# Joining the block inverses of a delta-rule layer: small products of different blocks issued in turn, matrix by matrix

## The chip, the cores and the metric

One core of one Trainium2 chip. The time is device microseconds of one execution of the whole program. The kernel before took 2122.88 us (median of three runs, 2118.37 to 2123.48).

## What is computed

A backbone with two layers over 512 latent and 256 context tokens of width 1024. Each layer has a modulation by a condition vector, an RMS norm, one input projection whose columns feed three groups of heads (latent attention, 2-D neighbourhood attention, a bidirectional gated delta rule), an output projection, and a SwiGLU. The change lies in the delta rule, in the inverse of a unit triangular matrix for every chunk, head and direction:

```
L = jnp.where(strict, jnp.einsum('bhnid,bhnjd->bhnij', kb, k) * decay, 0.0)
eye = jnp.eye(DN_CHUNK, dtype=f32)
tinv = lax.linalg.triangular_solve(L + eye, jnp.broadcast_to(eye, L.shape), left_side=True,
                                   lower=True, unit_diagonal=True)
u = tinv @ (v * beta[..., None])
w = tinv @ (kb * jnp.exp(gc)[..., None])
...
def step(S, xn):
    v_new = xn[0] - xn[1] @ S
    S_new = S * xn[3][..., None, None] + jnp.swapaxes(xn[2], -1, -2) @ v_new
```

The kernel works with chunks of 128 tokens: six chunks (four latent, two context), four heads, two directions, so 48 inverses of 128x128 a layer.

## The kernel before

The program runs on the five engines of one core under a scheduler. The Python code states tiles and operations; a list scheduler with a model of time writes the order in which each engine gets its instructions, and puts the semaphores. Code that is written in another order therefore also comes out elsewhere in the engines' lists.

Large projections split each float32 operand into a high and a low part (`wtiles`, L206, on ScalarE and GpSimd) and make three products for one (`mm3`, L107). All products are issued through `mm` (L103), so the profile shows them at L104 and tells them apart by their tiles. The small products of this change are plain float32, and each leaves two load and two matmul records in the trace.

The inverses are made in three steps. `base_inverse` (L664) inverts the 32x32 blocks on the diagonal of all matrices by substitution on VectorE and writes them to the tile `ST` ("strips"). `inverse` (L916) joins them into 128x128 inverses, first 32-blocks to 64-blocks, then 64-blocks to 128. One call takes two chunks, thus eight matrices (`R8`) in both directions, and is called for `x0` = 0, 2 and 4 in each layer: six calls in all. `scan` (L1014) then runs the recurrence over the chunks with the joined inverses `Yt`.

In `inverse` the 128 partitions hold four blocks of 32 (`B4`), or two halves of 64 (`fst`, `snd`). `LP` is the strictly triangular matrix, loaded by two transfers of four matrices each. Five groups of products follow each other, with copies out of PSUM between them:

- `pp` (L933 to L935): 32 products of 32x32, block `b` in, block `b ^ 1` out, copied to `p32` by ScalarE (L948);
- `xq` (L949 to L951; a half of the same PSUM tile as `pp`, so the profile calls it `pp<-p,strips`): 16 products of 32x32, blocks 1 and 2, copied into `X` by VectorE (L953);
- `pp64` (L958 to L960; `pp<-X,LP` in the profile): 16 products of 64x64, from one half to the other, copied to `p64` by VectorE and ScalarE (L962, L963);
- `yq` (L965 to L968): 32 products of 32x32, copied into `Y` by ScalarE (L970);
- `yq64` (L972 to L975; `yq<-Y,p`): 16 products of 64x64, each half copied into `Y` by ScalarE (L975).

In every group the loop over blocks is outermost and that over the eight matrices innermost: eight products in a row have the same rows and columns of the array, with other operands. All products of a group write one PSUM tile, each block its own partitions.

The first call in a layer runs beside the last projections (`TAIL`, `do_z`, `do_kv`, `do_ql`). The second and third run beside neighbourhood attention (`attention`, L847: `s_na`, `tp_na`, `o_na`) and the scans (`ks`, `yp`, `sp`, `qs`, `oa`), which `beside` (L1099) interleaves by a table; in layer 0 also beside the products of the modulation (`acc_ada`, from `ada_cols`, L220). `acc_ada` writes four strips of 32 columns in turn (`g = 32 * (k % 4)`). Loads for all of them are issued on SP's queue: `LP` (L922), the scan's `vp`, `kt`, `At` and `z` (L1011), `wada` (L225).

Of the kernel before, what the change touches and what calls it, by code (L numbers as in the profile page):

```python
# [102 lines left out]
def mm(nc, out, lhsT, rhs, start=True, stop=True):  # L103
    nc.tensor.matmul(out, lhsT, rhs, start=start, stop=stop)  # L104
# [16 lines left out]
def h4(t):  # L121
    return t.rearrange("p (h d) -> p h d", h=4)
# [240 lines left out]
def layer(tc, nc, a, l, es_x, xT, env, nx):  # L363
# [14 lines left out]
    def eb(name):  # L378
        tag = EB_TAG.get(name, "e")
        return psE.tile([P, 512], F32, tag=tag, name=name, bufs=EB[tag])  # L380
# [535 lines left out]
    def inverse(x0, sb, eb):  # L916


        LP = []
        for x in (x0, x0 + 1):  # L920
            LP.append(h4(sb.tile([P, 512], F32, tag="lLP", name="LP", bufs=2)))
            nc.sync.dma_start(out=LP[-1], in_=h4(d_LP[x]))  # L922
        Ys = [ST[:, 24 * d + 4 * x0:24 * d + 4 * x0 + 8] for d in range(2)]
        R8 = range(8)
        i8 = lambda t, c: t.rearrange("p (x c) -> p x c", c=c)
        f2 = lambda t: t.rearrange("p x c -> p (x c)")
        mix = sb.tile([P, 8, 32], F32, tag="mix", name="mix", bufs=1)
        for b in range(4):
            V.transpose(out=f2(mix[B4[b]]), in_=f2(Ys[b % 2][B4[b]]))
        q2 = eb("pp")  # L930
        pp, xq = i8(q2[:, 0:256], 32), i8(q2[:, 256:512], 32)
        for b in range(4):
            o = b ^ 1  # L933
            for x in R8:
                mm(nc, pp[B4[o], x], LP[x // 4][B4[b], x % 4, B4[o]], mix[B4[b], x])  # L935

        X = sb.tile([P, 8, 2, 32], F32, tag="X", name="X", bufs=1)
        for b in range(4):
            V.transpose(out=X[B4[b], :, b % 2], in_=f2(Ys[b // 2][B4[b]]))
        G.memset(X[B4[0], :, 1], 0.0)  # L940
        G.memset(X[B4[3], :, 0], 0.0)
        Y = []
        for d in range(2):
            Y.append(sb.tile([P, 8, 4, 32], F32, tag="Y", name=f"Y{d}", bufs=4 if x0 else 2))
            G.tensor_tensor(out=Y[d], in0=Ys[d].unsqueeze(2).to_broadcast([P, 8, 4, 32]),
                            in1=bm.unsqueeze(1).to_broadcast([P, 8, 4, 32]), op=ALU.mult)
        p32 = sb.tile([P, 8, 32], F32, tag="mix", name="p32", bufs=1)
        S.copy(out=p32, in_=pp)  # L948
        for b in (1, 2):  # L949
            for x in R8:  # L950
                mm(nc, xq[B4[b], x], Ys[1 - b % 2][B4[b], x], p32[B4[b], x])  # L951
        for b in (1, 2):
            V.tensor_copy(out=X[B4[b], :, 1 - b % 2], in_=xq[B4[b]])  # L953
        Xh = X.rearrange("p x b c -> p x (b c)")
        Yf = [t.rearrange("p x b c -> p x (b c)") for t in Y]
        pp = i8(eb("pp64"), 64)
        hf = ((fst, snd), (snd, fst))
        for a_, b_ in hf:  # L958
            for x in R8:
                mm(nc, pp[b_, x], LP[x // 4][a_, x % 4, b_], Xh[a_, x])  # L960
        p64 = sb.tile([P, 8, 64], F32, tag="X", name="p64", bufs=1)
        V.tensor_copy(out=p64[:, 0:4], in_=pp[:, 0:4])  # L962
        S.copy(out=p64[:, 4:8], in_=pp[:, 4:8])  # L963
        yq = i8(eb("yq")[:, 0:256], 32)
        for b in range(4):  # L965
            o = b ^ 1
            for x in R8:
                mm(nc, yq[B4[o], x], p32[B4[b], x], Ys[1 - b % 2][B4[b], x])  # L968
        for d, r, c in ((0, 0, 1), (0, 2, 3), (1, 1, 0), (1, 3, 2)):
            S.copy(out=Y[d][B4[r], :, c], in_=yq[B4[r]])  # L970
        yq = i8(eb("yq64"), 64)
        for d, (a_, b_) in enumerate(hf):  # L972
            for x in R8:
                mm(nc, yq[a_, x], p64[b_, x], Yf[d][b_, x, b_])
            S.copy(out=Yf[d][a_, :, b_], in_=yq[a_])  # L975
        for x in range(2):
            Yt[x0 + x] = [t[:, 4 * x:4 * x + 4] for t in Yf]

    es_si = ExitStack()
    sb_i = pool(es_si, f"sb_i{l}", side=B_)  # L980
    inverse(0, sb_i, att_bank)
    if "n" in TAIL[l]:
        open_na()
# [89 lines left out]
    def finish(c, tok, o):  # L1073
# [13 lines left out]
        for h in range(4):  # L1087
            PE.transpose(tp[:, HS[h]], o[:, HS[h]], ident)

        stt(out=qT[:, :, tok], in0=h4(tp), scalar=sml[:, 12:13], in1=h4(z), op0=ALU.mult, op1=ALU.mult)  # L1090

    I_, S_ = (lambda x: lambda: inverse(x, sb, eb)), (lambda d, x: lambda: scan(d, x))
    dn = iter([S_(0, 0), S_(1, 1), S_(0, 1), S_(1, 0), I_(2), S_(0, 2), S_(1, 3), I_(4), es_v.close,
               S_(0, 4), S_(1, 5), S_(0, 5), S_(1, 4), S_(0, 3), S_(1, 2)])
# [372 lines left out]
```

## Time and profile before

| | |
|---|---|
| median of three runs | 2122.88 us (2118.37 to 2123.48) |
| the profiled execution, its time | 2125.45 us |
| its span from first to last instruction | 2123.6 us |
| mean granted TensorE clock | 0.968 |
| TensorE (PE) busy | 1990.2 us, 94%, 12770 matmul records |
| VectorE (DVE) | 1172.3 us, 55% |
| ScalarE (ACT) | 714.3 us, 34% |
| GpSimd (POOL) | 758.7 us, 36% |
| 16 DMA engines, mean rate | 110 GB/s |

Busy times are shares of the whole span. Matmuls overlap each other in the array, so a matmul record is longer than the distance between two starts, and a busy PE is not a PE at its peak. In the timeline a row with "x16" is a group of 16 records, from the start of the first to the end of the last. In the chain of waits a piece counts from where the piece before it ends.

### The profile page before, as it was taken

To read this page: it belongs to the slowest core of one execution; us is meant where nothing else is said; L and a number is where in the kernel's file an instruction comes from. 1 tells how busy PE (TensorE), PEld (TensorE's weight loads), DVE (VectorE), ACT (ScalarE), POOL (GpSimd) and SP (SyncE) were. 2 spreads that over 40 slices of the span, in tenths; PEclk is the share of its full clock that TensorE was granted. 3 is DMA by queue.
4 is the path that set the end of the run, shared out by engine and by line. 5 is a ranking of instruction groups with operands and counts; after the bars stand their busy time and mean duration, and the time that the engine had idled before them with its cause. 6 is when DMAs were issued, how large, how long until landed. Compare 5 with 4: busy or idle time off the path is not lost. (4 is left out here: it accounts for less than half of the span.)

```text
span 2123.6 us, 32023 instructions
## 1 busy us (share of the span) xinstructions
PE 1990.2 (94%) x12770; PEld 1684.4 (79%) x12770; DVE 1172.3 (55%) x2045; ACT 714.3 (34%) x1385; POOL 758.7 (36%) x540
## 2 busy tenths in 40 slices
PE   6999998998998999999999988888998889999998
PEld 4788787887787888888888876767787678888887
DVE  4888813667656457246443268894568753212123
ACT  5433322334544221122122244333434543222233
POOL 3466132104322222322222443823311353444444
PEclk9999998999999999999999999999999999999999
DMA  7324252543322345344442331334232231333332
GB/s 279 82 76 153 81 157 77 168 149 112 104 64 78 109 126 165 97 130 131 128 129 76 121 95 55 119 120 124 91 88 77 87 95 60 99 99 94 95 97 92
DMA packets 119309, 232.56 MB, mean 110 GB/s; under 512 B 30516, under 2 KB 55988, under 8 KB 119032
## 3 DMA queue, kind: packets, MB, share of 16 engines
q1 hardware_dynamic: 119160, 230.51, 34.9%
q8 instruction: 101, 1.65, 0.3%
q14 instruction: 48, 0.39, 0.1%
HBM read 199.46 MB, written 31.01 MB: 109 GB/s over the span
## 5 line engine op out<-in xcount | busy, mean ns | idle before, releaser
L217 POOL TENSOR_TENSOR wl<-wr,wh 128x1024 fp32r<-128x1024 f32 (+2 forms) x188 | 442.0, 2352 | 848.4 <-ACT wh L216 834.9
L216 ACT CAST wh<-wr 128x1024 fp32r<-128x1024 f32 (+2 forms) x190 | 193.5, 1019 | 713.0 <-PE acc_gu L104 287.6
L104 PE MATMUL acc_gu<-fh,wh 128*128 128x512 f32 (+1 forms) x1024 | 359.1, 353 | 9.5 <-ACT fh L304 8.7
L104 PE MATMUL acc_gu<-fl,wh 128*128 128x512 f32 (+1 forms) x1024 | 361.0, 353 | 4.1 <-DVE fl L305 4.1
L104 PE MATMUL acc_gu<-fh,wl 128*128 128x512 f32 (+1 forms) x1024 | 360.2, 352 | 0.0
L104 PE MATMUL acc_in<-hh,wh 128*128 128x512 f32 (+1 forms) x640 | 230.5, 364 | 18.6 <-ACT xp L491 6.9
L104 PE MATMUL acc_in<-hl,wh 128*128 128x512 f32 (+1 forms) x640 | 229.9, 360 | 3.2 <-DVE hl L305 2.0
L104 PE MATMUL acc_in<-hh,wl 128*128 128x512 f32 (+1 forms) x640 | 227.3, 359 | 3.4 <-POOL wl L217 3.4
L104 PEld LDWEIGHTS acc_gu<-fh,wh 128*128 128x128 f32 x1024 | 194.1, 190 | 37.5 <-ACT fh L304 10.9
L1348 DVE TENSOR_TENSOR av<-acc_gu,av 128x768 f32<-128x768 f32 (+1 forms) x44 | 36.3, 825 | 338.4 <-PE acc_gu L104 330.0
L104 PEld LDWEIGHTS acc_gu<-fl,wh 128*128 128x128 f32 x1024 | 195.0, 190 | 30.3 <-DVE fl L305 4.3
L104 PEld LDWEIGHTS acc_gu<-fh,wl 128*128 128x128 f32 x1024 | 194.9, 190 | 26.3
L104 PEld LDWEIGHTS acc_in<-hh,wh 128*128 128x128 f32 x640 | 126.1, 198 | 45.4 <-ACT xp L491 8.6
L104 PE MATMUL acc_d<-al,wh 128*128 128x512 f32 (+1 forms) x444 | 157.2, 354 | 0.0
L104 PE MATMUL acc_d<-ah,wh 128*128 128x512 f32 (+1 forms) x444 | 157.2, 354 | 0.0
L104 PE MATMUL acc_d<-ah,wl 128*128 128x512 f32 (+1 forms) x444 | 156.1, 354 | 0.0
L254 DVE CUSTOM_DVE_ANT_0 junk<-wada,scb 128x1024 f32<-128x1024 f32 x112 | 145.3, 1297 | 6.8 <-DMA wada<-w_adaT 4.0
L104 PEld LDWEIGHTS acc_in<-hl,wh 128*128 128x128 f32 x640 | 127.0, 198 | 25.2 <-DVE hl L305 4.6
L104 PEld LDWEIGHTS acc_in<-hh,wl 128*128 128x128 f32 x640 | 126.1, 198 | 22.8 <-POOL wl L217 4.7
L1366 DVE SCALAR_TENSOR_TENSOR xT<-acc_d,mod,xT 128x512 f32<-128x512 f32 (+1 forms) x76 | 46.5, 634 | 155.2 <-PE acc_d L104 155.2
L501 DVE SCALAR_TENSOR_TENSOR cy<-xp,cw,cy 128x770 f32<-128x770 f32 (+1 forms) x96 | 117.7, 1226 | 20.5 <-ACT cy L499 18.5
L1352 DVE TENSOR_TENSOR al<-av,ah 128x768 fp32r<-128x768 f32 (+1 forms) x44 | 100.4, 2282 | 35.1 <-ACT ah L1351 35.1
(391 smaller groups left out, 3857.0 us busy)
## 6 DMA issues: line engine op xcount, KB each, us to landing
wr<-w_gu SPq DMA_DIRECT2D x88, 512.0 KB, 3.5
wada<-w_adaT SPq DMA_DIRECT2D x56, 512.0 KB, 3.4
wr<-w_in SPq DMA_DIRECT2D x48, 512.0 KB, 3.6
wr<-w_dn SPq DMA_DIRECT2D x32, 448.0 KB, 3.3
wada<-w_ada SPq DMA_DIRECT2D x24, 512.0 KB, 3.4
wada<-w_ada SPq DMA_DIRECT2D x8, 1024.0 KB, 8.1
wr<-w_dn SPq DMA_DIRECT2D x16, 512.0 KB, 3.5
xT<-xT SPq DMA_DIRECT2D x16, 384.0 KB, 4.9
```

What stands on the lines that cost most here:

```text
L104: nc.tensor.matmul(out, lhsT, rhs, start=start, stop=stop)
L216: S.copy(out=hi[:, sl], in_=raw[:, sl])
L217: eng.tensor_tensor(out=lo[:, sl], in0=raw[:, sl], in1=hi[:, sl].bitcast(F32), op=ALU.subtract)
L254: V.tensor_tensor_reduce(out=junk, in0=w, in1=scb[:, s], scale=1.0, scalar=0.0, op0=ALU.mult, op1=ALU.add, accum_out=mod[l][:, part, j, s: ...
L501: stt(out=y[:, :wid], in0=xp[:, j:j + wid], scalar=w_(j), in1=y[:, :wid], op0=ALU.mult, op1=ALU.add)
L1348: tt(out=av[:, :nT], in0=accs[1][:, :nT], in1=av[:, :nT], op=ALU.mult)
L1352: after.append(tt(out=l_[:, :nT], in0=av[:, :nT], in1=h_[:, :nT].bitcast(F32), op=ALU.subtract))
L1366: stt(out=xT[:, m, st_], in0=acc, scalar=mod[l][:, 5, m, s:s + 1], in1=xT[:, m, st_], op0=ALU.mult, op1=ALU.add)
```

## The change

In the five groups the loops change places: the matrices `x` are outermost and the blocks innermost, so that neighbouring products belong to different blocks. In `yq64` the two copies come after all 16 products, not each after its eight. Products, operands, tiles and transfers stay the same.

```diff
@@ -929,9 +929,10 @@
         q2 = eb("pp")
         pp, xq = i8(q2[:, 0:256], 32), i8(q2[:, 256:512], 32)
-        for b in range(4):
-            o = b ^ 1
-            for x in R8:
+
+        for x in R8:
+            for b in range(4):
+                o = b ^ 1
                 mm(nc, pp[B4[o], x], LP[x // 4][B4[b], x % 4, B4[o]], mix[B4[b], x])
@@ -946,8 +947,8 @@
         S.copy(out=p32, in_=pp)
-        for b in (1, 2):
-            for x in R8:
+        for x in R8:
+            for b in (1, 2):
                 mm(nc, xq[B4[b], x], Ys[1 - b % 2][B4[b], x], p32[B4[b], x])
@@ -955,23 +956,24 @@
         hf = ((fst, snd), (snd, fst))
-        for a_, b_ in hf:
-            for x in R8:
+        for x in R8:
+            for a_, b_ in hf:
                 mm(nc, pp[b_, x], LP[x // 4][a_, x % 4, b_], Xh[a_, x])
...
         yq = i8(eb("yq")[:, 0:256], 32)
-        for b in range(4):
-            o = b ^ 1
-            for x in R8:
+        for x in R8:
+            for b in range(4):
+                o = b ^ 1
                 mm(nc, yq[B4[o], x], p32[B4[b], x], Ys[1 - b % 2][B4[b], x])
...
         yq = i8(eb("yq64"), 64)
+        for x in R8:
+            for d, (a_, b_) in enumerate(hf):
+                mm(nc, yq[a_, x], p64[b_, x], Yf[d][b_, x, b_])
         for d, (a_, b_) in enumerate(hf):
-            for x in R8:
-                mm(nc, yq[a_, x], p64[b_, x], Yf[d][b_, x, b_])
             S.copy(out=Yf[d][a_, :, b_], in_=yq[a_])
```

How it moves TensorE's instructions is read from the order in which the two built programs list them. First, TensorE in layer 0, the end of the first joining, beside the projection of a z tile; `yq_2653` is `yq64`, `Y_2572` and `Y_2574` are the two directions. Before:

```order
L104 MATMUL acc_in<-hh_125,wl 128x512
L104 MATMUL yq_2653<-Y_2572,p_2613 64x64 x8
L104 MATMUL acc_in<-hh_126,wh 128x512
L104 MATMUL acc_in<-hl_134,wh 128x512
L104 MATMUL acc_in<-hh_126,wl 128x512
```

Now:

```order
L104 MATMUL acc_in<-hh_125,wh 128x512
L104 MATMUL acc_in<-hl_133,wh 128x512
L104 MATMUL acc_in<-hh_125,wl 128x512
L104 MATMUL yq_2653<-Y_2572,p_2613 64x64
L104 MATMUL yq_2653<-Y_2574,p_2613 64x64
```

Before, the eight products of the second direction stood 22 products of the projection further down. Now the two directions alternate, one product each, and all 16 stand together ahead of `acc_in<-hh_126`.

Second, TensorE in layer 1, the start of the second joining, beside attention and scans; `pp<-mix` is `pp`, `pp<-p_13967` is `xq`, `pp_13987` is `pp64`. Before:

```order
L104 MATMUL pp<-mix,LP 32x32 x22
L104 MATMUL sp<-w,kt 128x128 x4
L104 MATMUL pp<-mix,LP 32x32 x10
L889 MATMUL tp_na<-cst_61,pr 128x128 x8
L104 MATMUL yp<-vp,Y_13119 128x128 x4
L104 MATMUL pp<-p_13967,strips 32x32 x14
L104 MATMUL o_na<-pt,nav 64x128
L104 MATMUL pp<-p_13967,strips 32x32 x2
```

Now:

```order
L104 MATMUL yp<-vp,Y_13117 128x128 x4
L104 MATMUL pp<-mix,LP 32x32 x32
L104 MATMUL sp<-w,kt 128x128 x4
L889 MATMUL tp_na<-cst_61,pr 128x128 x8
L104 MATMUL pp<-p_13967,strips 32x32 x16
L104 MATMUL yp<-vp,Y_13119 128x128 x4
L104 MATMUL o_na<-pt,nav 64x128 x8
L104 MATMUL pp_13987<-X,LP 64x64 x16
```

The scan's `sp` stood inside `pp` and now follows it; `xq` and `pp64` stand unbroken, and `yp` comes after `xq`. Elsewhere in the two attention stretches pieces of the joining and of the scans change places in the same way.

## Rows read from the trace of the kernel before

**Rows 1.** The page: engines' busy times, and the chain by engine.

```profile
PE 1990.2 (94%) x12770; PEld 1684.4 (79%) x12770; DVE 1172.3 (55%) x2045; ACT 714.3 (34%) x1385; POOL 758.7 (36%) x540
...
PE 29%; DVE 6%; POOL 1%; ACT 1%; DMA 1%; issue 1%; SPq 0%; DVEq 0%; ACTq 0%; POOLq 0%
```

**Rows 2.** Busy time by stretch: length, busy us of each engine (instructions), clock, DMA.

```profile
281.00:375.00 94.00, 83.76 (x655) 70.92 (x654) 29.41 (x71) 27.14 (x58) 29.67 (x16) 0.85 0.37 107
375.00:470.00 95.00, 95.00 (x1234) 79.60 (x1233) 64.12 (x214) 33.09 (x115) 11.93 (x19) 1.00 0.49 158
...
1525.00:1592.00 67.00, 63.69 (x792) 56.36 (x793) 45.48 (x112) 24.92 (x73) 17.37 (x14) 0.95 0.32 97
```

**Rows 3.** Chain of waits, 1470 to 1600 us: start, us, engine, tile, line.

```profile
1479.90 1.84 PE pp L104 x64
...
1486.72 1.02 PE pp L104 x32
...
1492.73 1.83 PE pp L104 x32
1494.56 1.84 PE yq L104 x64
...
1503.19 1.07 PE yq L104 x16
...
1509.41 1.07 PE yq L104 x16
```

**Rows 4.** TensorE's waits, 1525 to 1592 us: total us, times, longest.

```profile
PE sp L104 <- DVE w L1035: 2.8, 1, 2.8
```

**Rows 5.** TensorE's waits, 318 to 376 us.

```profile
PE tr_ada L104 <- DVE adarow L231: 4.3, 2, 3.8
PE ms_q L104 <- DVE sqs L775: 3.5, 1, 3.5
```

**Rows 6.** Timeline, groups of small products: start us, us, operation, tiles, count.

```profile
295.09 1.91 PE L104 MATMUL pp<-mix,LP 32*32 32x32 f32 x64
...
301.60 1.09 PE L104 MATMUL pp<-p,strips 32*32 32x32 f32 x32
...
306.21 1.90 PE L104 MATMUL pp<-X,LP 64*64 64x64 f32 x32
...
379.44 0.50 PE L104 MATMUL pp<-mix,LP 32*32 32x32 f32 x10
...
386.28 0.37 PE L104 MATMUL pp<-mix,LP 32*32 32x32 f32 x6
...
416.78 1.02 PE L104 MATMUL yq<-Y,p 64*64 64x64 f32 x14
...
418.63 0.32 PE L104 MATMUL yq<-Y,p 64*64 64x64 f32 x2
...
420.36 1.14 PE L104 MATMUL yq<-Y,p 64*64 64x64 f32 x16
```

**Rows 7.** Timeline, products on four column strips and on the full array.

```profile
339.98 0.30 PE L104 MATMUL acc_ada<-wada,sc 128*32 128x128 f32 x1
...
339.98 0.32 PE L104 MATMUL acc_ada<-wada,sc 128*32 128x128 f32 x4
...
377.01 0.64 PE L104 MATMUL acc_ada<-wada,sc 128*32 128x128 f32 x16
...
1563.33 1.16 PE L104 MATMUL yp<-rr,Y 128*128 128x128 f32 x8
```

**Rows 8.** Busy time in two stretches at a lower clock, columns as in rows 2.

```profile
310.32:313.73 3.41, 3.41 (x14) 3.05 (x13) 0.13 (x1) 2.74 (x7) 0.44 (x1) 0.50 0.00 0
...
1498.16:1501.57 3.41, 3.41 (x10) 2.63 (x9) 0.34 (x2) 3.37 (x5) 0.00 (x0) 0.50 0.01 2
```

**Rows 9.** Groups by shape, 1470 to 1600 us: busy us, mean ns of one record.

```profile
L104 PE MATMUL pp<-mix,LP 32*32 32x32 f32 x192 | 6.6, 197 | 0.0
...
L104 PE MATMUL pp<-X,LP 64*64 64x64 f32 x96 | 6.1, 222 | 0.0
```

## Prediction

> **What bounds the kernel now.** I read the page first, then the busy time by stretch around the six joinings, then the chain of waits there, then TensorE's waits, and last the timeline of the small products. On the page TensorE is busy 94% of the span and has the largest share of the chain that ended last [rows 1]. That is a mean over stages, so the stretches decide. The second and third joining of layer 0 lie in 375 to 470 us, where TensorE is busy 95.00 of 95.00 us and VectorE 64.12; those of layer 1 lie in 1525 to 1592, with TensorE at 63.69 of 67.00 us and VectorE at 45.48. The first joining of each layer stands among projections; for layer 0 that is 281 to 375 us [rows 2]. In layer 1 the chain shows the products of the first joining themselves: 1.84 + 1.02 + 1.83 + 1.84 + 1.07 + 1.07 = 8.67 us of the chain for one joining [rows 3]. Six joinings run, so some 52 us of chain are at stake: TensorE is what ends last, and shorter products there should shorten the span. The limits of this: TensorE waits 2.8 us for VectorE's w in 1525 to 1592 [rows 4], and 4.3 and 3.5 us for VectorE after the first joining of layer 0 [rows 5].
>
> **What the small products cost now.** Each float32 product leaves two records, so `pp` with 32 products is a group of 64. Groups of one block give the pace within a block: 6 records take 0.37 us and 10 take 0.50, so a further record costs 0.13 / 4 = 0.0325 us. For 64-blocks, 2 records take 0.32 us and 14 take 1.02: 0.058 us each [rows 6]. All of `pp` at the pace of one block would take 0.50 + 54 x 0.0325 = 2.25 us, but its row says 1.91. It holds three passages from one block to the next, so each saves 0.34 / 3 = 0.115 us, the time of 3.5 records. Products of two blocks thus already run beside each other at a passage, 7 records in the time of 3.5, which is 0.016 us a record. The two blocks differ in rows and in columns of the array and write other partitions of the same PSUM tile.
>
> A row for four at once is `acc_ada`, whose products go in turn to four 32-column strips: 16 records with 128 columns take 0.64 us and four take 0.32, so 0.32 / 12 = 0.027 us a record. `yp`, on the full array with the same 128 columns, takes 8 records in 1.16 us, about 0.12 a record. The first record of an `acc_ada` group takes 0.30 us and the first four together 0.32, so starts 0.007 us apart are possible [rows 7].
>
> **The change, term by term.** Nothing is added or removed: 112 products for each joining before and after. The scheduler cuts them into 63 groups by the order listing, as many as before. What changes is that neighbours now belong to different blocks. If each block keeps its pace and the blocks run beside each other, a group lasts as long as one block's share of it, plus a step of 0.007 us for each further block.
> - `pp` (32 products, four blocks): one block has 16 records, 0.50 + 6 x 0.0325 = 0.70 us, with three steps 0.72. Against 1.91: 1.19 us saved.
> - `xq` (16 products, two blocks): 0.70 against 1.09: 0.39.
> - `pp64` (16 products, two halves): a half has 16 records, 1.14 us, with its step 1.15. Against 1.90: 0.75.
> - `yq` (32 products, four blocks, 64 records as in `pp`): 1.19.
> - `yq64`: two groups of 1.07 us on the chain become one of 1.08 [rows 3]: 1.06.
>
> That is 4.58 us for a joining and 27.5 us for six. The unknown is how closely four blocks can follow each other when a record is only 0.0325 us long. No row of before has that. Its bounds: the starts 0.007 us apart of `acc_ada` allow the full 27.5. At the 0.016 us of the passages, `pp` and `yq` would be 64 x 0.016 and the 0.197 us of a record [rows 9], 1.22 us, and save 0.69 each, in all 3.58, for six 21.5 us. At the 0.027 us that `acc_ada` keeps up, they would save nothing (64 x 0.027 + 0.197 = 1.92), `xq` 0.04, and the 64-blocks, two at 0.058 and so 0.029 us a record, all of theirs: 1.85, for six 11.1 us. I take 27.5, because the four strips of `acc_ada` are the row nearest in the number of neighbours, and their pace there is what one strip's 128 columns need.
>
> Edits that cost nothing here: the copies of both halves of `yq64` on ScalarE now wait for all 16 products, at most 0.6 us later than the first did. ScalarE is busy 33.09 of 95.00 us there [rows 2], and the first reader, a scan's `yp`, stands several products further on TensorE. If that cover is gone it costs 0.6 us a joining, 3.6 in all. With matrices outermost, the second of the two loads of `LP` is first needed halfway through `pp` instead of after four products, so SP's queue gets a little more time. Transfers of the scans (`vp`, `kt`, `At`) change places with those of `LP` and `w_ada` on SP as TensorE gets on faster; no wait for one of these is among TensorE's largest [rows 4, 5].
>
> From 27.5 I give back 3 us, the size of the 2.8 us wait on VectorE [rows 4]: with 9.2 of the 67 us gone from layer 1's stretch (two joinings), the scan's way through VectorE is what comes late next. That leaves 24.5 us. The profiled execution took 2125.45 us (span 2123.6), so 2101.0 by its own time. It lies 2.6 us above the median of the runs, 2122.88, so the forecast for the median is **2098.4 us**.
>
> **What the clock may add.** After `pp64` and `yq` of the first joining, the granted clock is 0.50 from 310.32 to 313.73 us and, in layer 1, from 1498.16 to 1501.57 [rows 8]. That is the lower of the two levels (1.2 and 2.4 GHz), each time after 1.83 + 1.84 us of small products [rows 3]. With that stretch cut to half, the fall may not come: each is worth half of 3.41, 1.7 us, together 3.4. I leave it out of the sum and in the range.
>
> **The rivals.**
>
> *Starts cannot follow closer than about 0.027 us.* For it: that is the steady pace of `acc_ada`, and nothing in the trace is steadily faster. Against it: passages at 0.016 us, and starts at 0.007. It gives 11.1 us, so 2111.8. The Trainium skill, "TensorE: Matmul & The Clock Gate", Part 1, says that starts of matmuls never come below about 25 ns however few columns they have. The passages of this trace lie below that, but only for a few records at a time.
>
> *The new order gives the gain back.* The list that TensorE follows is written by a scheduler, and in the two attention stretches it is a different one: scan products stand earlier or later between the pieces of the joining. A scan product whose VectorE input is late holds up all that stands behind it. The price of one such wait is 2.8 to 4.3 us [rows 4, 5], so seven new ones would eat the 24.5. Against it: TensorE loses hardly anything in 375 to 470 us now, and VectorE has 30.88 us free there. The time would lie within 6.4 us of before, about 2120. It also stands for the case that the scheduler does not keep the blocks in turn within `pp`, `xq` and `yq`, which the listing's names do not show.
>
> *Blocks of different rows cannot write one PSUM tile at once.* Then each product waits for the one before it to end. A record lasts 0.197 us for 32-blocks and 0.222 for 64-blocks [rows 9], so a product would take 0.197 + 0.0325 = 0.23 us instead of 1.91 / 32 = 0.06, and 0.28 instead of 0.119: 80 x 0.17 + 32 x 0.16 = 18.7 us more for a joining, 112 for six, 2235 us. It makes the kernel slower from the point at which one passage costs more than the next product gains. Against it stands the 0.115 us that each passage of `pp` saves, with all blocks in one PSUM tile. The Trainium skill, "TensorEngine Tiling (Array Packing)", Restrictions and Gotchas, states this rule: different row tiles cannot access the same PSUM bank simultaneously. The passages of this trace speak against it.
>
> **How the numbers follow.** Chances: forecast 0.58, starts at 0.027 us 0.18, gain given back 0.18, blocks shutting each other out 0.06. The range goes down to 27.5 + 3.4 for the clock + 3 for a kinder order, 34 us, so 2089, and up through the second case with 6 us given back to the order, to 2118. It leaves out the last case and most of the third. Measurement can tell 0.3%, 6.4 us. Faster by more than that: 0.58 + 0.18 + 0.02 of the third case = 0.78. Within it: 0.13 of the third. Slower: the remaining 0.03, and 0.06: 0.09.
>
> **What would show it.** In the timeline after, an unbroken `pp` or `yq` of 64 records should take about 0.7 us instead of 1.91, `pp64` and `yq64` of 32 about 1.15. If `pp` takes about 1.2, the pace of the passages holds for four; if 1.9, the second case; if far more, the last. The stretch from the first attention product to the last scan should shrink by some 10 us in each layer; if the groups shrink and the stretch does not, new waits for VectorE should stand before `sp`, `yp` or `s_na`. The half-clock stretches after the first joining should be gone. The forecast is wrong if the groups shrink as said and the time does not follow within 6 us.

## The result, and the profile after

The changed kernel takes 2106.43 us, median of four runs (2104.68 to 2107.70); the kernel before, beside it, 2122.14 (four runs, 2118.37 to 2123.48). The ratio is 0.9924 with a 95% interval of 0.9903 to 0.9945: 15.7 us faster, where 24.5 were forecast (2098.4). The profiled execution took 2107.7 us, with a span of 2105.9: 17.7 us less than the span before. The page of the kernel after, TensorE's busy time and the chain by engine, to be held against [rows 1]:

```profile
PE 1960.6 (93%) x12770; PEld 1656.1 (79%) x12770; DVE 1183.1 (56%) x2045; ACT 714.5 (34%) x1385; POOL 760.6 (36%) x540
...
PE 27%; DVE 7%; DMA 2%; ACT 2%; POOL 1%; issue 1%; SPq 0%; DVEq 0%; ACTq 0%; POOLq 0%
```

The records are the same in number. TensorE is busy for 29.6 us less, VectorE for 10.8 us more with the same 2045 instructions: something besides the products has changed.

**The products.** The timeline of the kernel after, the first joining of layer 0 (start us, us, operation, tiles, count), answers to [rows 6]:

```profile
296.49 0.75 PE L104 MATMUL pp<-mix,LP 32*32 32x32 f32 x64
...
301.85 0.69 PE L104 MATMUL pp<-p,strips 32*32 32x32 f32 x32
...
306.49 1.14 PE L104 MATMUL pp<-X,LP 64*64 64x64 f32 x30
307.56 0.74 PE L104 MATMUL yq<-strips,p 32*32 32x32 f32 x62
...
313.16 1.15 PE L104 MATMUL yq<-Y,p 64*64 64x64 f32 x32
```

The prediction had 0.72 us for `pp` and `yq`, 0.70 for `xq`, 1.15 for `pp64`; `yq64` is one group of 1.15. The blocks of different rows and columns run beside each other, all writing one PSUM tile. The chain of waits of the kernel after for the first joining of layer 1 (start, us, engine, tile, line), against [rows 3]:

```profile
1470.53 0.68 PE pp L104 x50
...
1476.42 0.62 PE pp L104 x32
...
1482.03 0.26 PE pp L104 x2
1482.29 0.17 PE yq L104 x2
1482.46 1.07 PE pp L104 x30
1483.53 0.67 PE yq L104 x49
...
1489.41 1.08 PE yq L104 x32
```

That is 4.55 us for one joining instead of 8.67: 4.12 saved, 4.58 forecast. `pp`, `xq` and `yq64` saved 1.16, 0.40 and 1.06 as worked out (1.19, 0.39, 1.06). `pp64` and `yq` now stand wound into each other, and each piece pays its entry: 0.50 and 1.00 in place of 0.75 and 1.19. Summed over all groups of both layers, from the start of a group's first record to that of its last (a pause of over 0.3 us parts a group), the small products fell from 47.7 to 22.7 us: 25.0 us (27.5 forecast).

**The stages.** The busy time by stretch, with columns as in [rows 2], cut at landmarks that TensorE passes in every version: from the start to the first `acc_gu` (the SwiGLU of layer 0), from layer 1's `gc` to its first `acc_v` (projections, ahead of any joining), and from layer 1's first `pp` to its first `acc_gu` (joinings, scans, both attentions). The kernel before:

```profile
0.00:669.90 669.90, 605.14 (x4575) 501.21 (x4575) 435.82 (x884) 263.72 (x602) 236.40 (x212) 0.95 0.38 121
1300.70:1421.20 120.50, 110.26 (x589) 88.97 (x589) 102.46 (x137) 46.21 (x73) 68.05 (x59) 0.96 0.35 112
1421.20:1479.80 58.60, 48.16 (x271) 41.62 (x271) 35.21 (x76) 17.72 (x33) 18.09 (x10) 0.88 0.46 126
1479.80:1740.60 260.80, 242.24 (x2137) 204.28 (x2136) 165.45 (x382) 114.59 (x305) 77.56 (x69) 0.97 0.29 86
```

The kernel after:

```profile
0.00:653.30 653.30, 586.01 (x4574) 485.44 (x4574) 444.01 (x883) 264.57 (x602) 236.49 (x212) 0.96 0.40 125
1283.80:1409.60 125.80, 110.78 (x589) 88.69 (x590) 106.59 (x139) 46.33 (x73) 70.07 (x59) 0.95 0.33 108
1409.60:1470.50 60.90, 50.45 (x279) 43.53 (x280) 33.92 (x74) 18.26 (x33) 17.95 (x10) 0.86 0.44 120
1470.50:1723.20 252.70, 228.51 (x2133) 189.74 (x2133) 165.87 (x382) 113.22 (x305) 78.35 (x69) 0.97 0.29 89
```

Layer 0 gained 16.6 us and layer 1 from `pp` on 8.1, together 24.7. That is close to what the products became shorter by, but only as a sum: by layer they fell by 12.5 and 12.4 us. And 7.6 us are lost between `gc` and `pp` of layer 1 (120.5 + 58.6 to 125.8 + 60.9), 5.3 of them in 120 us of projections where no product of the change stands. The rest of the program differs by 0.6 us. So the question for the experiments was what these projections have to do with the change.

TensorE's waits in layer 1 of the kernel after, the first line from the projections (1283.8 to 1409.6), the others from 1470.5 to 1723.2:

```profile
PE acc_in L104 <- ACT xp L491: 8.0, 2, 7.5
...
PE s_mla L104 <- ACT pr L1208: 4.6, 3, 3.8
PE yp L104 <- DVE rr L1032: 4.1, 2, 3.5
```

The same of the kernel before (1300.7 to 1421.2, and 1479.8 to 1740.6):

```profile
PE acc_in L104 <- ACT xp L491: 5.0, 2, 4.2
...
PE yp L104 <- DVE rr L1030: 4.3, 2, 3.5
```

The wait for `xp` grew by 3.0 us, and a wait of latent attention's `s_mla` for ScalarE, 4.6 us, is new. TensorE waits for no copy into `Y` in either trace, so the later copies of `yq64` show no cost.

**The clock.** Two stretches of the kernel after, around the places of [rows 8], columns as in [rows 2]:

```profile
306.00:313.50 7.50, 7.50 (x134) 6.34 (x134) 0.85 (x2) 4.44 (x8) 2.33 (x1) 1.00 0.05 16
1481.90:1492.00 10.10, 10.10 (x166) 8.65 (x166) 3.40 (x9) 7.73 (x14) 0.00 (x0) 1.00 0.18 54
```

Both stretches at the lower level are gone, but others came and went. From the start to `acc_gu` the granted clock is 0.50 for 62.6 us before and for 57.2 us after, over the whole execution for 136.0 and 129.4 us. If each us there costs half a us, 6.6 us less of it are worth up to 3.3 us of the 17.7 (an estimate).

### The profile page after: what moved, and what is told of

Its sections match the earlier page's. It is cut to its first block, busy times and chain, and to the rows that moved or that the text cites. A ratio compares the mean times of both kernels' runs of the same rounds, so it can differ in the third digit from the quotient of the medians.

```text
span 2105.9 us, 32048 instructions
## 1 busy us (share of the span) xinstructions
PE 1960.6 (93%) x12770; PEld 1656.1 (79%) x12770; DVE 1183.1 (56%) x2045; ACT 714.5 (34%) x1385; POOL 760.6 (36%) x540
## 5 line engine op out<-in xcount | busy, mean ns | idle before, releaser
L104 PEld LDWEIGHTS acc_in<-hh,wh 128*128 128x128 f32 x640 | 124.6, 196 | 46.1 <-ACT xp L491 10.8
L501 DVE SCALAR_TENSOR_TENSOR cy<-xp,cw,cy 128x770 f32<-128x770 f32 (+1 forms) x96 | 123.4, 1285 | 23.9 <-ACT cy L499 20.5
```

The source lines that it names most:

```text
L501: stt(out=y[:, :wid], in0=xp[:, j:j + wid], scalar=w_(j), in1=y[:, :wid], op0=ALU.mult, op1=ALU.add)
```

## Experiments

All stretches from the profiled executions, in us; "sum" is that of the groups of small products. "At 0.50" is the time at the lower clock level within two of these stretches, start to `acc_gu` and, in layer 1, `pp` to `acc_gu`. The last column says which of two orders layer 1's projections came out in: b, in which TensorE's records stand as in the kernel before (but for at most one), or a, as in the changed one.

| kernel | median time | ratio to before (95%) | sum | start to `acc_gu` | `gc` to `acc_v` | `pp` to `acc_gu`, layer 1 | at 0.50 | order |
|---|---|---|---|---|---|---|---|---|
| before | 2122.14 | | 47.7 | 669.9 | 120.5 | 260.8 | 62.6, 17.1 | b |
| after | 2106.43 | 0.9924 (0.9903 to 0.9945) | 22.7 | 653.3 | 125.8 | 252.7 | 57.2, 13.7 | a |
| e1 | 2130.95 | 1.0048 (1.0030 to 1.0066) | 48.8 | 661.9 | 125.9 | 264.5 | 51.2, 30.7 | a |
| e2 | 2104.30 | 0.9916 (0.9900 to 0.9932) | 22.1 | 656.6 | 120.0 | 255.9 | 61.1, 20.5 | b |
| e3 | 2117.94 | 0.9979 (0.9965 to 0.9992) | 36.4 | 651.9 | 125.7 | 268.8 | 52.9, 41.0 | a |
| e4 | 2112.97 | 0.9959 (0.9946 to 0.9972) | 34.6 | 669.5 | 120.7 | 253.5 | 62.5, 13.7 | b |
| e5 | 2109.86 | 0.9951 (0.9938 to 0.9965) | 33.1 | 654.1 | 126.4 | 260.9 | 54.6, 37.5 | a |
| e6 | 2122.21 | 1.0011 (0.9996 to 1.0027) | 37.9 | 665.1 | 126.3 | 258.2 | 69.1, 13.7 | a |
| e7 | 2096.38 | 0.9881 (0.9865 to 0.9898) | 22.1 | 651.9 | 120.2 | 253.2 | 49.1, 13.7 | b |
| e8 | 2099.94 | 0.9899 (0.9884 to 0.9914) | 21.9 | 655.9 | 119.8 | 250.1 | 51.3, 10.2 | b |
| e9 | 2093.70 | 0.9871 (0.9849 to 0.9892) | 21.8 | 649.7 | 119.7 | 251.2 | 51.5, 13.7 | b |
| e10 | 2128.95 | 1.0040 (1.0023 to 1.0058) | 48.6 | 663.0 | 126.5 | 262.6 | 58.0, 27.3 | a |

The kernel before took 2121.09 us beside e1 to e4, 2120.87 beside e5 to e8, and 2121.30 beside e9 and e10.

Each stretch comes from one execution, and the granted clock differs from one execution to the next. The ten of e3 ran from 2111.79 us, at a mean granted clock of 0.971, to 2121.40 at 0.964; the ten of e6 from 2116.59 at 0.970 to 2131.91 at 0.961. So a few us between two orders are not shown to be the order's where the clock differs too. In layer 0, before and e4 have one and the same order of TensorE's records by line, tile and shape, and so have after and e3, e2 and e8, e7 and e9: these pairs lie 0.4 to 2.2 us apart.

### e1: block by block as before, in another order of blocks

The kernel before, with `pp`'s blocks from the last to the first. No product goes in turn; the list comes out in order a in layer 1's projections.

```diff
-        for b in range(4):
+        for b in (3, 2, 1, 0):
             o = b ^ 1
             for x in R8:
                 mm(nc, pp[B4[o], x], LP[x // 4][B4[b], x % 4, B4[o]], mix[B4[b], x])
```

> The kernel before, block by block as ever, but pp takes its blocks as 3, 2, 1, 0. The products keep their pace, but the scheduler then lists TensorE's instructions of layer 1's projections exactly as in the changed kernel (154 rows unlike the kernel before). Theory (part of the gain is lost to that other order): the stretch from layer 1's gc to its first pp takes 186 to 188 us as in the changed kernel, not 179, and the whole is 5 to 8 us slower than before, about 2129. Rival (that stretch was long by chance of the run, or since layer 1 starts 17 us earlier): 179 us, and about 2122.

Its busy time by stretch, columns as in [rows 2]:

```profile
0.00:661.90 661.90, 600.11 (x4574) 498.01 (x4574) 437.15 (x882) 264.14 (x601) 232.89 (x211) 0.96 0.38 122
1295.10:1421.00 125.90, 111.21 (x589) 89.08 (x590) 106.87 (x139) 46.39 (x73) 69.58 (x59) 0.95 0.33 108
1478.50:1743.00 264.50, 247.85 (x2134) 209.21 (x2133) 166.16 (x382) 113.40 (x305) 78.25 (x69) 0.94 0.27 85
```

With the old products and the new order the projections of layer 1 take 125.9 us, as after the change, and VectorE is busy for 106.87 us there, also as after (106.59; before 102.46). So these 5 us do not come from the turn, but from the order. From `gc` to `pp` it is 183.4 us, not the 186 to 188 expected: the other 2.3 us of the changed kernel, between `acc_v` and `pp`, are not there (57.5 us against 60.9), so they are none of this order. A change with no use of its own costs 0.48%; its executions had a granted clock of 0.961 to 0.969, those of before beside them 0.964 to 0.972, so a part of that can be the clock's.

### e2: the change, with layer 1's projections in the order of before

```diff
         for x in R8:
-            for b in range(4):
+            for b in (0, 2, 1, 3):
                 o = b ^ 1
                 mm(nc, yq[B4[o], x], p32[B4[b], x], Ys[1 - b % 2][B4[b], x])
```

> The changed kernel with yq's blocks in turn as 0, 2, 1, 3. Every group still goes in turn, and the scheduler lists layer 1's projections exactly as in the kernel before. Theory: the stretch from layer 1's gc to its first pp takes 179 us again instead of 186.7, and the whole is 5 to 8 us faster than the changed kernel, 2098 to 2102. Rival: it stays near 186 us and the whole near 2106.

Its busy time by stretch:

```profile
0.00:656.60 656.60, 586.58 (x4575) 485.34 (x4575) 439.88 (x884) 263.94 (x602) 236.64 (x212) 0.95 0.39 124
1286.80:1406.80 120.00, 109.53 (x589) 88.19 (x589) 102.11 (x137) 46.15 (x73) 68.04 (x59) 0.96 0.35 112
1464.50:1720.40 255.90, 232.50 (x2137) 192.75 (x2136) 165.46 (x382) 113.69 (x305) 78.26 (x69) 0.96 0.28 88
```

The projections are back at 120.0 us with all products in turn: e1 and e2 together settle that stretch. The whole, 2104.30 us, missed the expected 2098 to 2102 and gained only 2.1 us on the changed kernel. Layer 0 has another order too and is 3.3 us longer. Layer 1 from `pp` on is 3.2 longer, though TensorE's order there differs from the changed kernel's in only 21 of some 2130 records; e4 and e7, with the order of e2, took 253.5 and 253.2 us. Where the projections' 5 us sit is seen in the groups of VectorE by line, one row of the kernel after (1283.8 to 1409.6):

```profile
L501 DVE SCALAR_TENSOR_TENSOR cy<-xp,cw,cy 128x512 f32<-128x512 f32 (+1 forms) x32 | 40.9, 1278 | 2.2 <-ACT rk L589 1.4 <-ACT cy L499 0.3
```

and the same of e2 (1286.8 to 1406.8):

```profile
L501 DVE SCALAR_TENSOR_TENSOR cy<-xp,cw,cy 128x512 f32<-128x512 f32 (+1 forms) x32 | 36.2, 1132 | 1.1 <-ACT cy L499 0.6
```

The same 32 steps (half of them of 128x512, half of 128x770) take 4.7 us longer in order a, and `xp`, which feeds them, holds TensorE up for longer: 8.0 us, against 5.2 in e2. Which neighbours make them longer wasn't tried, but the two traces point at GpSimd. The steps with nothing on GpSimd beside them took 0.74 to 0.75 us (128x512) and 1.00 to 1.02 (128x770). All that took over 1.1 us, 13 in order a and 10 in e2, had GpSimd instructions beside them for about half of their time or more, though a few that had them were not longer. GpSimd and, beside it, the longest 128x512 step of the kernel after, in the timeline:

```profile
1297.94 2.49 POOL L217 TENSOR_TENSOR wl<-wr,wh 128x1024 fp32r<-128x1024 f32 x1 [6.95 <-ACT wh L216]
...
1298.28 2.70 DVE L501 SCALAR_TENSOR_TENSOR cy<-xp,cw,cy 128x512 f32<-128x512 f32 x1
```

### e3 and e4: the change in one layer alone

`l == 0` in e3, `l == 1` in e4, in all five groups; the first is shown.

```diff
-        for b in range(4):
-            o = b ^ 1
-            for x in R8:
-                mm(nc, pp[B4[o], x], LP[x // 4][B4[b], x % 4, B4[o]], mix[B4[b], x])
+        for b, x in ([(b, x) for x in R8 for b in range(4)] if l == 0 else [(b, x) for b in range(4) for x in R8]):
+            o = b ^ 1
+            mm(nc, pp[B4[o], x], LP[x // 4][B4[b], x % 4, B4[o]], mix[B4[b], x])
...
```

> In turn in layer 0 only; layer 1 block by block. Layer 1's projections are listed as in the changed kernel. Theory: layer 0's joining stretch gives 19 us, the projections of layer 1 take 7.6 back, so about 2111. Rival (the loss is none of the order): 2103. If the gain of a joining comes from its own products alone, the joining stretch of layer 1 stays at 110 us.

> In turn in layer 1 only. Everything ahead of layer 1's first joining is listed as in the kernel before. Theory: 179 us from gc to the first pp, the joining stretch of layer 1 gives 14.7 us, and the latent attention behind it, listed as in the changed kernel, takes 6.5 back: about 2114. Rival (the losses are none of the order): the projections take 186 us, about 2121, or the latent attention loses nothing, about 2107.

e3's stretch of layer 1, block by block but in a new order:

```profile
1466.10:1734.90 268.80, 254.58 (x2134) 213.57 (x2133) 165.28 (x382) 113.66 (x305) 78.57 (x69) 0.92 0.27 84
```

e4 came out as expected, e3 did not: 2117.94 instead of 2111. Layer 0 has all its gain (651.9 against 653.3). But layer 1, with the old products, takes 268.8 us where the kernel before took 260.8. The joinings of layer 1, from `pp` to the first product of latent attention (`acc_mv`), in the kernel before:

```profile
1479.80:1589.70 109.90, 105.58 (x1201) 89.98 (x1201) 61.53 (x160) 46.46 (x117) 28.78 (x21) 0.95 0.28 84
```

and in e3:

```profile
1466.10:1585.00 118.90, 116.80 (x1216) 99.56 (x1215) 63.52 (x164) 46.14 (x118) 29.45 (x22) 0.87 0.26 82
```

TensorE is busy there nearly throughout, at a granted clock of 0.87 against 0.95: 30.7 us at the lower level, 10.2 before. The 20.5 us more are worth up to 10 us by themselves (an estimate), which is more than the 8 us that are missing. The executions of e3 at a clock of 0.969 or above took 2111.79 to 2114.57 us. So it is not shown that the order costs 8 us in the joinings; the clock alone could account for them. Why it was lower stays open.

### e5 and e6: one kind of block alone

In e5 `pp`, `xq` and `yq` go in turn, in e6 `pp64` and `yq64`; the others stand block by block. From the changed kernel, e5 undoes:

```diff
-        for x in R8:
-            for a_, b_ in hf:
+        for a_, b_ in hf:
+            for x in R8:
                 mm(nc, pp[b_, x], LP[x // 4][a_, x % 4, b_], Xh[a_, x])
...
```

and `yq64` in the same way; e6 undoes the other three.

> Only the 32-block groups (pp, xq, yq) go in turn; pp64 and yq64 stay block by block, with the copies of yq64 after each eight. Theory (each kind of product is worth its own shortening, whatever the other does): the first-to-last-start sum of the 32-block groups falls from 26.6 us to about 11 in both layers together, that of the 64-block groups stays at 21.2; -15.6 us of TensorE time, of which about 5 are lost again because the projections of layer 1 come out in the same order as after the change (stretch from the first gc to the first acc_v of layer 1 at 125.8 us). About 2110, the joining of layer 0 at 188 us, that of layer 1 at 102. Rival (the time follows the order that the scheduler finds, not the length of the products): the joining stretches do not shrink by 8 us each, time anywhere from 2105 to 2122.

> Only the 64-block groups (pp64, yq64) go in turn; pp, xq and yq stay block by block. Theory: the sum of the 64-block groups falls from 21.2 us to about 11.8, that of the 32-block groups stays at 26.6; -9.4 us, of which about 5 are lost to the order of layer 1's projections (first gc to first acc_v 125.8 us). About 2117, joining of layer 0 at 192 us, of layer 1 at 105. Rival (the gain hangs on the order): joining stretches away from these by more than 4 us. If e5 and e6 together gain less than the whole change, the two kinds are not worth their sum.

Timeline of e5, the first joining of layer 0:

```profile
294.84 0.75 PE L104 MATMUL pp<-mix,LP 32*32 32x32 f32 x64
...
304.42 1.90 PE L104 MATMUL pp<-X,LP 64*64 64x64 f32 x32
```

and of e6:

```profile
296.61 1.91 PE L104 MATMUL pp<-mix,LP 32*32 32x32 f32 x64
...
308.16 1.14 PE L104 MATMUL pp<-X,LP 64*64 64x64 f32 x30
```

Each kind shortens by itself: the sums are 33.1 us (14.6 less) and 37.9 (9.8 less), together 24.4 of the 25.0. The joinings of e5, 186.3 and 105.4 us, and of e6, 190.5 and 104.8, lie within 3.4 us of what was expected. In time e5 met its expectation (2109.86 for 2110), e6 missed it by 5 (2122.21 for 2117). With the 5.3 us of order a added to each, e5 gains 16.3 us, e6 4.0, and the whole change 21.0: within the width of the intervals the two kinds add up. By itself, though, e6 gained less in time than its products became shorter by, 4.0 for 9.8 us, at a granted clock of 0.961 to 0.970; how much of the rest is the clock and how much the order stays open.

### e7: the change, with another order of pp's blocks

```diff
         for x in R8:
-            for b in range(4):
+            for b in (0, 2, 1, 3):
                 o = b ^ 1
                 mm(nc, pp[B4[o], x], LP[x // 4][B4[b], x % 4, B4[o]], mix[B4[b], x])
```

> The whole change, with pp's blocks in the order 0, 2, 1, 3 within each matrix: the same products in turn, another order from the scheduler in both joinings and in layer 1's latent attention, the same in layer 1's projections. Theory (length of the products is fixed by the turn, the rest is order): sum of the groups 22 to 23 us as after the change, first gc to first acc_v 125.8 us; joinings at 178 and 95 us, each within 5; latent attention of layer 1 anywhere from 88 to 97. 2101 to 2111. Rival (the turn itself lengthens layer 1's latent attention, by VectorE or by crowding): that stretch again 94 to 97.

The expectation was wrong about the order: the list has order b in layer 1's projections, and in layer 1's latent attention that of the changed kernel, so only layer 0 and the projections were moved, and 2096.38 lies below the range. The latent attention, 94.9 us from `acc_mv` to `acc_o`, therefore tells nothing between theory and rival. Its busy time by stretch:

```profile
0.00:651.90 651.90, 583.12 (x4574) 482.99 (x4574) 441.23 (x884) 264.80 (x602) 236.53 (x212) 0.96 0.39 125
1283.20:1403.40 120.20, 109.97 (x588) 88.60 (x589) 102.38 (x137) 46.27 (x73) 68.07 (x59) 0.96 0.34 112
1461.70:1714.90 253.20, 230.41 (x2136) 190.04 (x2136) 165.54 (x382) 113.92 (x305) 78.32 (x69) 0.97 0.28 89
```

With the projections in order b and 1.4 us less in layer 0, the change gives 2096.38 us: 24.5 us under the kernel before beside it, and 10 us under the changed kernel, with the same products.

### e8: another table for the scans of layer 1

e2, with the table that gives out the steps of the delta rule beside layer 1's attention:

```diff
-DNS = ([1, 0, 0] + [1] * 4 + [0] + [1] * 12, [2, 2, 2, 1, 1, 2, 3] + [2] * 11)
+DNS = ([1, 0, 0] + [1] * 4 + [0] + [1] * 12, [2, 2, 2, 2, 2, 2, 3] + [2] * 11)
```

> As e2 (the change, yq's blocks in the order 0, 2, 1, 3, layer 1's projections in the order of the kernel before), but the table that gives out layer 1's scans beside attention reads 2, 2, 2, 2, 2, 2, 3 where it read 2, 2, 2, 1, 1, 2, 3. The joinings keep their order but for one product; 72 places in layer 1's latent attention change. Theory (the 6.7 us given back in layer 1's latent attention are a matter of order): that stretch, 96.7 us in e2, moves by more than 3 us with nothing else moving; if down to 88 to 90, the time is 2096 to 2098. Rival (scans have only moved out of a shorter joining, and whatever the order they need this long): it stays at 94 to 97 and the time at 2104.

Layer 1 from `pp` to `acc_gu`:

```profile
1463.90:1714.00 250.10, 228.49 (x2137) 189.38 (x2136) 165.22 (x382) 114.41 (x305) 78.36 (x69) 0.98 0.29 90
```

The latent attention stays at 94.5 us, as the rival had it, but that decides little: by line, tile and shape TensorE's 583 records there stand in the same order as in e2, and nearly all that the table moved lies behind them. In all six kernels with layer 1 in turn (after, e2, e4, e7 to e9) this one order stands there, and the stretch takes 94.0 to 96.7 us, against 88.0 before. Its busy time by stretch, the kernel before:

```profile
1589.70:1677.80 88.10, 75.79 (x559) 63.40 (x557) 70.28 (x149) 40.80 (x129) 24.65 (x34) 0.96 0.24 68
```

and the kernel after:

```profile
1565.70:1660.30 94.60, 81.22 (x584) 67.99 (x584) 71.61 (x153) 40.97 (x129) 25.27 (x34) 0.95 0.23 66
```

`s_mla` waits 4.5 to 4.8 us for ScalarE's `pr` in each of the six; in the kernel before, in e1 and in e10 that wait does not occur. Yet TensorE stands idle for only 1.1 us more in all (13.4 for 12.3 us): the new wait stands for the most part in place of others. The larger part, 5.4 of the 6.5 us, is busy time: 25 more records stand between these landmarks, and the clock is a little lower. Most of what seemed to be given back here is thus work that stood elsewhere before. Whether another order would shorten the stretch with all products in turn was not tried. With other records in it, it took 90.3 us (e1), 89.2 (e10), 95.5 (e3) and 98.5 (e5).

The time is 4.4 us under that of e2, but the intervals overlap, and from `pp` on e8 stood 10.2 us at the lower clock, e2 20.5.

### e9: the two best stages together

e7 with the table of e8.

> e7 (pp's blocks 0, 2, 1, 3, the change otherwise) with the table of e8 (scans of layer 1 given out 2, 2, 2, 2, 2, 2, 3). Theory (stages are worth their lengths one by one; a gain of order in one layer does not touch the other): layer 0 as in e7, start to first acc_gu 652 us; layer 1 from its first pp to its first acc_gu as in e8, 250 us; first gc to first acc_v 120; about 2093. Rival (e8's 250 against 253 to 256 was scatter of one execution): 253 or more, and 2096 as e7.

```profile
0.00:649.70 649.70, 582.32 (x4575) 483.31 (x4575) 441.93 (x884) 264.48 (x602) 236.86 (x212) 0.96 0.39 125
1279.60:1399.30 119.70, 109.33 (x588) 88.12 (x589) 102.26 (x137) 46.18 (x73) 68.05 (x59) 0.97 0.35 113
1457.30:1708.50 251.20, 229.19 (x2136) 190.75 (x2136) 165.27 (x382) 113.80 (x305) 77.99 (x69) 0.97 0.28 89
```

That is its busy time by stretch. 2093.70 us, with the forecast at 2093, and layer 0 keeps e7's length (649.7 us for 652). Layer 1 from `pp` on came out between theory and rival (251.2 us for 250, or 253 or more), and the interval overlaps with that of e7, so that the table is worth anything beside e7's order is not shown. It has the lowest median, 1.29% under before (0.9849 to 0.9892).

### e10: block by block in a third order

```diff
-        for b in range(4):
+        for b in (3, 2, 1, 0):
```

in `pp` and in `yq` of the kernel before.

> Block by block as before, with the blocks of pp and of yq in the order 3, 2, 1, 0: nothing in turn, a third order of the list for block by block. Theory (the turn is worth its shorter products, some 12.5 us a layer, as a mean over orders; which order a kernel gets moves each layer by some us either way): sum of the groups 47 to 50 us; start to first acc_gu 661 to 671 us (block by block so far 669.9, 669.5, 661.9; in turn 651.9 to 656.6), layer 1 from pp to acc_gu 260 to 269 (so far 260.8, 264.5, 268.8; in turn 250.0 to 255.8); 2120 to 2133. Rival (the order is worth as much as the turn): one of the two stretches falls among those of the kernels in turn.

Start to `acc_gu` and layer 1 from `pp`, its busy time by stretch:

```profile
0.00:663.00 663.00, 599.98 (x4575) 498.82 (x4575) 439.91 (x882) 265.18 (x601) 234.35 (x211) 0.96 0.38 122
...
1480.80:1743.40 262.60, 246.50 (x2134) 208.31 (x2133) 166.22 (x382) 113.99 (x305) 78.35 (x69) 0.95 0.28 86
```

Both lie among the block by block kernels, clear of those in turn. Taking kernels with one order in a layer together, layer 0 has three orders block by block (669.7, 661.9, 663.0; mean 664.9) and three in turn (652.6, 656.3, 650.8; mean 653.2); layer 1 from `pp` on has four (260.8, 264.5, 268.8, 262.6; mean 264.2) and three (252.7, 254.2, 250.7; mean 252.5). On these executions the turn is worth 11.7 us a layer, 23.4 in all, and the orders lie within 8 us of each other block by block and within 6 and 4 in turn. Two things limit this. In layer 1 some of these orders hardly differ: e1 and e10 in 8 of TensorE's records from `pp` on, after and e2 in 21, e2 and e8 in 172. And the clock goes along: in layer 1 the kernels block by block stood 29.0 us at the lower level on the mean, those in turn 13.9, in layer 0 57.2 and 53.8. At half a us for each that is up to 9 of the 23.4 us (an estimate). Whether the turn itself keeps the clock up was not tried apart.

## Why the prediction was right, and where not

- **The place** was right. The time comes out of the joinings of both layers, and TensorE was what ended last there: the stretches that hold the products shortened, in layer 0 where only layer 0 goes in turn (e3, 651.9 for 669.9 us), in layer 1 where only that does (e4, 253.5 for 260.8). That they shortened by 24.7 us and the products by 25.0 is in part luck: layer 0 gained 4 us more than its products, layer 1 4 us less. By kind, e5 and e6 show the shorter products; in time e5 bears them out, e6 only in part.
- **The length of the groups** was right: 0.75 us for 0.72, 0.69 for 0.70, 1.14 for 1.15. The term was 27.5 us and measured 25.0. The missing 2.5 come at least in part from groups that the list cuts: the working took `pp64` and `yq` as unbroken, and in the first joining of each layer they stand wound into each other (in layer 1 0.44 us of the 0.46 that one joining lacks).
- **The rival with starts no closer than 0.027 us** is refuted: 64 records begin within 0.56 us. **Blocks that shut each other out of one PSUM tile** is refuted by the same row.
- **The 3 us given back** is the step that failed. The prediction set it at the size of one wait on VectorE in the second and third joining. It had its size and its place wrong: 7.3 us were given back by the span (25.0 less 17.7), and the largest part, 5.3 us, lies in layer 1's projections, which the prediction did not look at, because nothing of the change stands there. e1 and e2 show its cause: the list there comes in two orders, and it changes with edits that have nothing to do with the products. Taking these 5.3 us off, the same change in order b would be at about 2101 (an estimate; e2 came to 2104.30, e7 to 2096.38).
- **The rival in which the new order gives the gain back** had the mechanism in part, with the wrong place and price: it asked for seven new waits in the attention stretches. One is there, `s_mla` on ScalarE, 4.6 us, but TensorE's idle time in that stretch grew by only 1.1 us.
- **The clock**: both named falls are gone, and over the whole execution the time at the lower level fell by 6.6 us, close to the 6.8 of the two falls, though by other falls coming and going. It was left out of the sum. What it gave, up to 3.3 us, cannot be told from the rest.
- **The prediction's own sign of being wrong** came up: the groups shrank as said, and the time lies 8.0 us from the forecast, where it allowed 6. The mechanism held, and the sum that ends in 2098.4 did not.

The time of 2106.43 us lies in the range (2089 to 2118). Kernels with the same products in turn came out anywhere from 2093.70 to 2106.43, clock included. So how near the middle a kernel with these products comes hangs on the clock and on an order that nobody chose; e7, at 2096.38, would have met it.

## What to carry to other kernels

Small products on different row and column blocks of the array should follow each other in turn: block by block each is held to the pace of its own block, in turn they overlap, here from 1.91 to 0.75 us for 64 records. Whether different rows or different columns alone would do was not tried. Where a scheduler writes the order, a change is to be judged stage by stage: a stage without any edit can shift by a third of the gain (5.3 of 15.7 us here), and an edit of no meaning (the order of the blocks) shows how much of a result is order. Read the granted clock of each stage first: with the order unchanged, executions of e3 and e6 at a lower one were up to 10 and 15 us longer. Then a few such harmless orders are worth trying for themselves: 2106 to 2094 us here with equal work.

## What the runs showed of the hardware

Of the products by shape in the kernel after (1440 to 1600 us; busy us, mean ns of one record):

```profile
L104 PE MATMUL pp<-mix,LP 32*32 32x32 f32 x192 | 2.6, 194 | 0.4 <-DMA LP<-d_LP 0.3
```

The group of 0.75 us, less one record of 0.194, has 64 starts in 0.56 us: 0.009 us from start to start, kept up over a whole group, on four blocks that differ in rows and columns and write different partitions of one PSUM tile. That is close to a quarter of the 0.0325 us that one block needs for a record; `xq`, on two blocks, comes to 0.016, half of it. So each block keeps nearly its own pace beside the others. A record lasts as long as before (0.197 us, [rows 9]). The Trainium skill, "TensorE: Matmul & The Clock Gate", Part 1, puts starts at no less than about 25 ns; this trace does not agree where the products lie on different blocks. Nor does the trace agree with what the Trainium skill states in "TensorEngine Tiling (Array Packing)", Restrictions and Gotchas, that different row tiles cannot access one PSUM bank at once, in the sense that would make these products wait for each other.

Not expected, either: VectorE's time for the same instructions depends on what stands beside them (1278 against 1132 ns for the 32 `cy` steps), so in this kernel its busy time is no fixed sum of its work.
